# Gated linear attention in an already tuned two-layer trunk: value products of 512 columns, attention products set among the projections, two levels with fewer key columns

## The chip, the cores and the metric

The kernel runs on one core of a Trainium2 chip. The metric is the device time of one execution in microseconds (us), as the median of several runs; the profile is one further execution, recorded by the hardware profiler.

## The reference

A trunk of two layers works on 512 tokens of width 1024, all in float32. Each layer has a token mixer and a gated convolutional feed-forward network (FFN, inner width 2816); around every sublayer stand an RMS norm of the input with a shift and scale (adaLN) and an RMS norm of the output with a gate. Layer 0 mixes tokens with an RG-LRU recurrence, layer 1 with gated linear attention (GLA), which is what the change touches:

```python
proj = h @ w_in
q, k, v, r, z = jnp.split(proj, [GLA_QK, 2 * GLA_QK, 2 * GLA_QK + D_MODEL, 2 * GLA_QK + 2 * D_MODEL], axis=-1)
log_alpha = jax.nn.log_sigmoid((z @ w_alpha + b_alpha)) / GLA_TAU
...
o_inter = jnp.einsum('bhcd,bhde->bhce', qc * jnp.exp(big_g), state)
attn = jnp.einsum('bhid,bhjd,bhijd->bhij', qc, kc, decay)   # decay = exp(G_i - G_j), causal
o_intra = jnp.einsum('bhij,bhje->bhie', attn, vc)
state = jnp.exp(g_last)[..., None] * state + jnp.einsum('bhjd,bhje->bhde', kc * jnp.exp(g_last - big_g), vc)
...
o = rmsnorm(o, norm_g)
return (o * jax.nn.silu(r)) @ w_out
```

There are four heads, with keys of 128 and values of 256.

## The kernel before, in words

Activations lie with channels on the 128 partitions and the 512 tokens along the free axis; `h` is eight tiles of 128 by 512. For accuracy every large product is done three times in the type float32r: the weight and the activation are each split into a high and a low part, and hi·hi, hi·lo and lo·hi are summed in PSUM (`mm3`, `mms`). Weights come from memory in units of 512 KB (`unit`, `load_upto`): a DMA of the SP queue into one of 3 raw slots, a cast on ScalarE (`acopy`, L416), a subtraction on VectorE (`tt`, L364), and the two parts lie in one of 8 slots of the pool `w`. Most other tiles come from a pool `g` of 43 slots; products go to 7 PSUM banks, `mm`.

Before it emits anything the program records all its operations and orders them with a list schedule in Python (`Sched.order`). TensorE takes the lowest recorded operation whose inputs are ready by the schedule's own reckoning, so it goes in recorded order except where something isn't ready; the other engines go by the longest path to the end. How long an operation takes in this reckoning is written in `Emit`: for products in `mms`. At run time each engine executes its list strictly in order and waits on semaphores. So a number in `mms` can move instructions in the whole program, not only in GLA.

In GLA, the projections of z, q and k come first. Then for each head in turn: a product for the diagonal of the 128 by 128 attention blocks (`diag_start`); the value projection (`vproj`), which holds 128 tokens of `h` stationary and moves 256 weight columns, 96 products; two blocks of the output gate `r` (`rproj`), which hold the weights and move 512 tokens, 48 products; seven levels of the decayed attention (`level_x` prepares on VectorE and ScalarE, `level_mm` multiplies four token blocks, in plain float32, and `masked` copies the result under a mask); the products between blocks (`inter_mm`); and `attend`, which multiplies attention and values and norms the result. A plain float32 product stands in the order once and in the profile twice, since the chip runs it in two passes.

Each output projection (`out_proj`) runs the two token halves one after the other and norms each: `rstd_bcast` sums squares over partitions with a product of one column per 128 tokens ("the sum", tile `nr`), computes the power on POOL, puts it on a diagonal on VectorE and broadcasts it by one more product (also `nr`, "the broadcast"). This happens for y and, with the next sublayer's input in view, for h: four norms per `out_proj`, whose two products each stand somewhere among the products of the other half. `h_tile` then makes the next input, and the next sublayer's first products need it (`proj_halves`).

Of the kernel before, what the change touches and what calls it, by code (L numbers as in the profile page):

```python
# [12 lines left out]
ALU = mybir.AluOpType  # L13
# [16 lines left out]

def unit_list():
    """Weight units in the order of their use: (key, array name, [(k, m), ...])."""
# [42 lines left out]
# column-parameter layout  # L75
# [10 lines left out]
class Buf:  # L86
    """A tile whose place on the chip is taken when its first instruction is emitted."""
# [10 lines left out]
class View:  # L98
# [41 lines left out]
class Sched:  # L140
    """Records the kernel's instructions with their operands, orders them by a list schedule
    (deadlines from the longest path to the end, the tensor engine in program order), and
    emits them to Tile in that order."""
# [34 lines left out]
    def order(self):  # L178
# [23 lines left out]
        # allocation order per class  # L202
# [29 lines left out]
        cand = {e: [] for e in ENGS}     # (prio, idx) ready or soon ready  # L232
        wait = {e: [] for e in ENGS}     # (ready, idx)
# [11 lines left out]
        while done < n:  # L245
# [8 lines left out]
            for e in ENGS:  # L254
# [7 lines left out]
                if e == "act" and cand[e]:  # L262
                    # a change of the function table costs time: prefer the present one
# [80 lines left out]
class Emit:  # L344
    """Instruction wrappers: costs and operands for the schedule, closures for the emission."""
# [118 lines left out]
def trunk(ctx, tc, xT, wall, adaT, par_d, c_d, walpha_d, ident_d, masks_d, outT):  # L464
# [57 lines left out]
    def load_upto(i):  # L522
        while nxt[0] <= min(i, len(UNITS) - 1):
# [9 lines left out]
            if UNITS[j][0] in ingen:  # L533
                # in general tiles, which are plenty at the start of a sublayer
# [8 lines left out]
            if UNITS[j][0][0] == "gz":  # L543
                # 16 columns of either part side by side: one product serves both
# [44 lines left out]
    def rstd_from(nr, nt, dim, act=False):  # L589
        """nr[:, :nt]: sums per token tile -> rstd broadcast to all partitions (PSUM)."""  # L590
# [38 lines left out]
    def mod_cols(layer, part, k0=0, k1=KD):  # L629
        """Finish a part: 0/3 shift, 1/4 (1+scale)*norm_g, 2/5 gate*norm_g."""  # L630
# [32 lines left out]
    def h_tile(h, k, sl, rb, n, layer, part_sh):  # L663
        """h = (x * s2) * rstd + shift, in two parts."""
# [7 lines left out]
    def out_proj(src, wkey, klist, gate, nexth, yacc=None):  # L672
        """Last product of a sublayer, y = src @ W (+ yacc); x += gate * rmsnorm(y) * g; then the
        next sublayer's h, or the output. The token halves follow each other, so that the norms
        of one run beside the products of the other."""
# [4 lines left out]
        for sl in HALVES:  # L680
            acc = s.buf("gh", F32, 256)
            ys = []
            for m in range(KD):
# [28 lines left out]
            if nexth is None and sl is HALVES[1]:  # L712
                # the tensor engine, idle by now, takes part of the sums
# [35 lines left out]
    def proj_halves(keys, h_):  # L749
        """First products of a sublayer, by token halves and input tiles as these become ready."""  # L750
# [79 lines left out]
    def ada_col(part, k):  # L830
        """One column of the first norm's shift or scale."""
# [419 lines left out]
```

## Time and profile before

| | |
|---|---|
| median of 3 runs | 1185.19 us (1184.75 to 1185.59) |
| span of the profiled execution, first to last instruction | 1182.5 us |
| TensorE busy | 1158.9 us, 98% of the span |
| VectorE, ScalarE busy | 867.3 us (73%), 553.6 us (47%) |
| granted TensorE clock, mean | 0.999 |
| GLA's value, gate and attention products | 608 to 756 us of the span |

The profiled execution's own time is not listed apart from its span; the median lies 2.7 us above the span. A row of the timeline reads: start, length, engine, line, operation, tiles written and read, the stationary block (rows*columns), the moving one, and how many follow each other; a matmul's end is modelled, so the distance of two starts says more than a length.

### The profile page before, as it was taken

The numbers are of one execution on the slowest core, as the hardware profiler recorded it, in microseconds if no ns is written. First come the engines' busy times: TensorE is split into PE (matmuls) and PEld (weight loads), VectorE is DVE, ScalarE is ACT, GpSimd is POOL, SyncE is SP. The second block draws the span as 40 slices with busy tenths as digits, with TensorE's granted clock in tenths as the row PEclk, the third lists the DMA queues.
The fourth block names the chain that finished last, engine by engine and source line by source line (L and its number), as shares of the span: only waits on it lengthen the run. The fifth ranks groups of instructions, "written<-read, shape, count | busy, mean of one in ns | idle before, by whom it ended". The sixth has DMA issues, their size and how long they took to land.

```text
span 1182.5 us, 16970 instructions
## 1 busy us (share of the span) xinstructions
PE 1158.9 (98%) x6664; PEld 1017.0 (86%) x6664; DVE 867.3 (73%) x1470; ACT 553.6 (47%) x874; POOL 24.4 (2%) x37
## 2 busy tenths in 40 slices
PE   4999999999999999999999999999999999999998
PEld 3878899988888888899999899999988888888897
DVE  7999999988988956558779767458845556645635
ACT  5688864743333324434478344254643333424421
POOL 1000001000000000000000000000000000000000
PEclk9999999999999999999999999999999999999999
DMA  8956562477787843232412211203243333332202
GB/s 338 312 170 202 200 214 73 160 249 252 249 260 223 261 126 93 88 90 59 144 55 90 72 54 55 72 27 118 72 125 97 100 91 105 90 107 90 72 1 72
DMA packets 45857, 157.44 MB, mean 133 GB/s; under 512 B 4977, under 2 KB 7281, under 8 KB 45778
## 3 DMA queue, kind: packets, MB, share of 16 engines
q1 hardware_dynamic: 45778, 156.36, 41.6%
q8 instruction: 52, 0.85, 0.3%
q14 instruction: 27, 0.22, 0.1%
HBM read 154.25 MB, written 2.10 MB: 132 GB/s over the span
## 4 chain that ended last, share of the span: by engine, by line
PE 90%; DVE 5%; ACT 3%; issue 1%; DMA 1%; SPq 0%; POOL 0%; DVEq 0%; POOLq 0%
PE mm L435 88%; ACT g L411 2%; PE nr L435 1%; DVE g L377 1%; DVE w L364 1%; ACT L411 1%; DVE g L364 1%; ACT w L416 1%; DVE gh L377 1%; DVE g L393 1%; DVE w L377 1%; DMA const<-in_xT_dram 0%; DMA raw<-in_wall_dram 0%; DVE araw L377 0%; SPq L441 0%
## 5 line engine op out<-in xcount | busy, mean ns | idle before, releaser
L435 PE MATMUL mm<-g,w 128*128 128x512 f32 (+1 forms) x5114 | 957.5, 348 | 5.6 <-ACT g L416 2.5
L435 PEld LDWEIGHTS mm<-g,w 128*128 128x128 f32 x5114 | 826.2, 189 | 130.4 <-ACT g L416 4.1
L364 DVE TENSOR_TENSOR w<-raw,w 128x1024 fp32r<-128x1024 f32 (+1 forms) x181 | 217.8, 1205 | 152.4 <-ACT w L416 152.0
L416 ACT CAST w<-raw 128x1024 fp32r<-128x1024 f32 (+1 forms) x181 | 187.2, 1036 | 206.3 <-PE mm L435 202.3
L377 DVE SCALAR_TENSOR_TENSOR g<-mm,const,g 128x511 f32<-128x511 f32 (+3 forms) x208 | 153.3, 745 | 11.2 <-ACT g L411 5.3
L364 DVE TENSOR_TENSOR g<-g,g 128x512 f32<-128x512 f32 (+4 forms) x213 | 126.2, 614 | 37.7 <-ACT g L411 19.4
L411 ACT ACTIVATE g<-mm,const 128x512 f32<-128x512 f32 (+1 forms) x148 | 102.2, 698 | 20.6 <-PE mm L435 20.5
L411 ACT ACTIVATE g<-g 128x512 f32<-128x512 f32 (+1 forms) x132 | 66.7, 540 | 96.2 <-DVE g L377 77.4
L435 PE MATMUL mm<-g,g 128*128 128x256 f32 (+4 forms) x748 | 102.1, 293 | 0.0
L435 PEld LDWEIGHTS mm<-g,g 128*128 128x128 f32 (+1 forms) x748 | 94.8, 191 | 3.8
L416 ACT CAST g<-g 128x512 fp32r<-128x512 f32 (+1 forms) x74 | 45.4, 614 | 107.7 <-DVE g L364 105.0
L377 DVE SCALAR_TENSOR_TENSOR araw<-araw,const 128x1024 f32<-128x1024 f32 x72 | 87.1, 1220 | 9.2 <-DMA araw<-in_adaT_dram 9.0
L364 DVE TENSOR_TENSOR g<-g,mm 128x512 f32<-128x512 f32 (+1 forms) x80 | 44.9, 577 | 44.5 <-PE mm L435 44.2
L364 DVE TENSOR_TENSOR gh<-gh,gh 128x256 f32<-128x256 f32 x97 | 40.4, 420 | 22.2 <-ACT gh L411 20.6
L435 PE MATMUL mm<-w,g 128*128 128x256 f32 x384 | 49.6, 288 | 0.0
L435 PEld LDWEIGHTS mm<-w,g 128*128 128x128 f32 x384 | 46.9, 192 | 1.4 <-issue 1.4
L368 POOL TENSOR_TENSOR sm<-sm,const 128x2 f32<-128x2 f32 (+1 forms) x19 | 19.4, 1022 | 1025.7 <-DVE sm L388 1018.5
L411 ACT ACTIVATE gh<-g 128x256 f32<-128x256 f32 x32 | 13.1, 416 | 51.3 <-DVE g L364 51.3
L411 ACT ACTIVATE g<-gh,const 128x256 fp32r<-128x256 f32 x48 | 21.9, 503 | 26.4 <-DVE gh L377 26.2
L411 ACT ACT_TABLE_LOAD x24 | 30.8, 1283 | 1.1 <-PEq L1242 0.7
L377 DVE SCALAR_TENSOR_TENSOR w<-w,const 128x1024 f32<-128x1024 f32 x24 | 28.8, 1217 | 0.0
L411 ACT ACTIVATE gh<-const 128x256 f32<-128x256 f32 x48 | 18.9, 414 | 20.1 <-DVE const L364 20.0
(66 smaller groups left out, 465.6 us busy)
## 6 DMA issues: line engine op xcount, KB each, us to landing
raw<-in_wall_dram SPq DMA_DIRECT2D x186, 512.0 KB, 3.7
araw<-in_adaT_dram SPq DMA_DIRECT2D x72, 512.0 KB, 4.5
w<-in_adaT_dram SPq DMA_DIRECT2D x24, 512.0 KB, 5.8
raw<-in_wall_dram SPq DMA_DIRECT2D x8, 384.0 KB, 6.7
const<-in_xT_dram SPq DMA_DIRECT2D x8, 256.0 KB, 4.1
out_dram<-const SPq DMA_DIRECT2D x8, 256.0 KB, 2.1
araw<-in_masks_dram SPq DMA_DIRECT2D x1, 512.0 KB, 5.2
const<-in_par_dram SPq DMA_DIRECT2D x1, 291.0 KB, 3.6
```

The source lines that it names most:

```text
L364: self.s.add(eng, dur, lambda: e.tensor_tensor(out.ap(), a.ap(), b.ap(), op=op), [a, b], [out])
L368: lambda: self.nc.gpsimd.tensor_tensor(out.ap(), a.ap(), b.ap(), op=ALU.pow), [a, b], [out])
L377: return self.nc.vector.scalar_tensor_tensor(out.ap(), a.ap(), f(sc), b.ap(), op0=op0, op1=op1, **kw)
L393: lambda: self.nc.vector.tensor_tensor_scan(out.ap(), a.ap(), b.ap(), 0.0, op0=ALU.mult, op1=ALU.add),
L411: return self.nc.scalar.activation(out.ap(), a.ap(), func, **kw)
L416: self.s.add("act", (0.095 if self._sb(a) else 0.052) + out.n * 0.8325e-3, lambda: self.nc.scalar.copy(out.ap(), a.ap()), [a], [out])
L435: r.append(self.nc.tensor.matmul(g[0].ap(), g[1].ap(), g[2].ap(), start=g[3], stop=g[4], **kw))
```

## The change

The value weights of two heads are laid side by side: a `gv` unit holds two input tiles by four column tiles, four units serve a pair of heads, and `vproj` makes one token block of 128 for both heads with products that move 512 columns. It holds the same `h` blocks stationary. A list, `GLA_CHUNKS`, fixes the order of 16 projections of 24 products each (8 of values, 8 of the gate); each head takes the next 6, 3, 5 and 2 of them, and its nine small steps (diagonal, seven levels, the products between blocks) are recorded evenly behind these. `level_mm` and `masked` leave out key columns that the mask clears anyway where that leaves 96 or fewer: 96 of 128 at level 32, 64 of 128 at level 64. `mms` charges other times: 11 ns more for each float32r product, and for plain float32 a time that depends on the columns moved and held. Comments are dropped, and lines are shifted by 6.

```diff
+GLA_CHUNKS = ([("v", t) for t in range(4)] + [("r", 0), ("r", 1), ("r", 2), ("r", 3), ("v", 4), ("v", 5),
+              ("v", 6), ("v", 7), ("r", 4), ("r", 5), ("r", 6), ("r", 7)])
+GLA_ENDS = (6, 9, 14, 16)
...
-    for h in range(NH):
-        for half in range(2):
-            u.append((("gv", h, half), "gla_w_in",
-                      [(4 * half + k, 8 + 2 * h + c) for k in range(4) for c in range(2)]))
-        for j in range(2):
-            u.append((("gr", 2 * h + j), "gla_w_in", [(k, 16 + 2 * h + j) for k in range(KD)]))
+    for what, i in GLA_CHUNKS:
+        if what == "r":
+            u.append((("gr", i), "gla_w_in", [(k, 16 + i) for k in range(KD)]))
+        elif i % NT == 0:
+            for quarter in range(4):
+                u.append((("gv", i // NT, quarter), "gla_w_in",
+                          [(2 * quarter + k, 8 + 4 * (i // NT) + c) for k in range(2) for c in range(4)]))
...
             if g[1].buf.dt == FR:
-                dur += max(n, 256) * 0.4167e-3 + 0.0025
+                dur += max(n, 256) * 0.4167e-3 + 0.0135
             else:
-                dur += max(n, 118 if n > 1 else 100) * 1.667e-3 + 0.005
+                dur += 2 * max(n * 0.8333e-3 + 0.002, 0.112 if g[1].n > 64 else 0.062)
...
+    def vproj(pair, t):
+        w = [unit("gv", pair, i) for i in range(4)]
+        ps = mmtile()
+        for k in range(KD):
+            ww, c = w[k // 2], (k % 2) * S
+            hh, hl = h[k]
+            whi, wlo = ww[c:c + S], ww[D + c:D + c + S]
+            tok = tsl(t)
+            e.mms([(ps[:], hh[tok], whi, k == 0, False), (ps[:], hl[tok], whi, False, False),
+                   (ps[:], hh[tok], wlo, False, k == KD - 1)])
+        vt[pair, t] = gt()
+        e.acopy(vt[pair, t][:], ps[:])
...
-        e.mms([(ps[t * n:(t + 1) * n], xt[tsl(t)], part3(xt[tsl(t)], 2 * hb, hb, 2 * hb), True, True)
-               for t in range(NT)])
-        masked(atd, lv, ps, 2 * hb, hb)
+        rows = P - hb
+        rows = rows if rows <= 96 else P
+        e.mms([(ps[t * n:(t + 1) * n].rows(rows), xt[t * P:t * P + rows], part3(xt[tsl(t)], 2 * hb, hb, 2 * hb),
+                True, True) for t in range(NT)])
+        masked(atd, lv, ps, 2 * hb, hb, rows)
...
     for hd in range(NH):
-        atd = diag_start(hd)
-        vproj(hd)
-        sr = rproj(hd)
-        for lv, hb in enumerate(LEVELS):
-            level_mm(atd, lv, level_x(hd, hb))
-        ax = inter_mm(inter_x(hd))
-        attend(hd, atd, ax, sr)
+        ats, axs = {}, {}
...
+        small = [start] + [lambda lv=lv: level(lv) for lv in range(len(LEVELS))] + [inter]
+        chunks = GLA_CHUNKS[done:GLA_ENDS[hd]]
+        done = GLA_ENDS[hd]
+        given = 0
+        for n, (what, i) in enumerate(chunks):
+            vproj(i // NT, i % NT) if what == "v" else rproj(i)
+            upto = len(small) * (n + 1) // len(chunks)
+            for f in small[given:upto]:
+                f()
+            given = upto
+        attend(hd, ats[0], axs[0])
```

The first place is TensorE in GLA's first head. Before, the seven levels follow each other behind the second gate projection (the row of 128x512); the row's last figures are the output block.

```order
L435 MATMUL mm_5923<-g_5152,w_5478 128x512
L435 MATMUL mm_5973<-g_5717 128x64 x4
L435 MATMUL mm_5980<-g_5725 128x64 x4
L435 MATMUL mm_5988<-g_5734 128x64 x4
L435 MATMUL mm_5995<-g_5759 128x64 x4
L435 MATMUL mm_6005<-g_5781 128x64 x4
L435 MATMUL mm_6013<-g_5795 128x64 x4
L435 MATMUL mm_6021<-g_5819 128x64 x4
L435 MATMUL mm_6033<-g_5761,g_5832 128x128
```

Now level 32 stands alone between two gate projections:

```order
L441 MATMUL mm_5977<-g_5172,w_5587 128x512
L441 MATMUL mm_5977<-g_5132,w_5587 128x512
L441 MATMUL mm_6016<-g_5764 96x64 x4
L441 MATMUL mm_6025<-g_5005,w_5615 128x512
L441 MATMUL mm_6025<-g_5022,w_5615 128x512
```

What moved: the levels stand in 14 groups behind a longer product in the four heads together, where they stood in 4; three of the groups are level 64 or begin with it, two begin with level 32.

The second place is TensorE where the first FFN ends and GLA's first products begin (rows of 32x256 are the product with the weights of z, the first that needs GLA's `h`; the `nr` row is the last norm's broadcast). Before, six products stand between the two:

```order
L435 MATMUL nr_5342<-gh_5367,const_82 128x256
L435 MATMUL mm_5138<-g_5142,w_4890 128x256
L435 MATMUL mm_5138<-g_5171,w_4890 128x256
L435 MATMUL mm_5138<-g_5142,w_4890 128x256
L435 MATMUL mm_5138<-g_5152,w_4890 128x256
L435 MATMUL mm_5138<-g_5181,w_4890 128x256
L435 MATMUL mm_5138<-g_5152,w_4890 128x256
L435 MATMUL mm_5098<-g_5028,w_4801 32x256
```

Now there are 24; the broadcast is followed by

```order
L441 MATMUL nr_5335<-gh_5360,const_82 128x256
L441 MATMUL mm_5149<-g_5126,w_4853 128x256
L441 MATMUL mm_5149<-g_5167,w_4853 128x256
L441 MATMUL mm_5149<-g_5126,w_4853 128x256
L441 MATMUL mm_5149<-g_5132,w_4853 128x256
L441 MATMUL mm_5149<-g_5172,w_4853 128x256
L441 MATMUL mm_5149<-g_5132,w_4853 128x256
L441 MATMUL mm_5155<-g_5077,w_4896 128x256
```

What moved: the norm's two products came forward past other work. The same holds before the first FFN: between the last broadcast of a half and the first product that needs `h`, 6 products became 36 in the first half and 12 became 30 in the second. Between the sum and the broadcast of the eight norms of the first two output projections stood 27, 24, 21, 24, 18, 18, 25 and 21 products; now 21, 18, 21, 18, 15, 18, 20 and 18.

The third place is VectorE in head 0, where the second pair's value weights are split (rows with `raw`; `COPY_PREDICATED` is a level's masked copy):

```order
L370 TENSOR_TENSOR w_5945<-raw_5637,w_5945 128x1024
L370 TENSOR_TENSOR w_5955<-raw_5689,w_5955 128x1024
L1078 COPY_PREDICATED g_5778<-const_5654,mm_5958 128x32x8
L1078 COPY_PREDICATED g_5778<-const_5654,mm_5968 128x16x16
L370 TENSOR_TENSOR w_5963<-raw_5853,w_5963 128x1024
L370 TENSOR_TENSOR w_6004<-raw_5966,w_6004 128x1024
L1078 COPY_PREDICATED g_5778<-const_5654,mm_6016 96x8x32
```

What moved: the four units of a pair are split together; these four stand among the copies of head 0, and the product that first reads one of them stands behind the attention of head 0 and two more gate projections. Before, two units of the next head stood about there.

More of the change, by code (lines that the diff above doesn't have):

```diff
@@ L1066, in bcol, with masked @@
         return v.map(lambda a: a.rearrange("p (n c) -> p n c", c=c)[:, :, j:j + 1].to_broadcast([P, v.n // c, c]))
-    def masked(atd, lv, ps, c, lo):
+    def masked(atd, lv, ps, c, lo, rows=P):
         def cut(v, t):
-            return v.ap().rearrange("p (t n c) -> p t n c", t=t, c=c)[:, :, :, lo:c]
+            return v.ap()[0:rows].rearrange("p (t n c) -> p t n c", t=t, c=c)[:, :, :, lo:c]
         n, k = P // c, c - lo
@@ L1075, in masked @@
         e.dve(0.07 + src.n * 1.042e-3, lambda: nc.vector.copy_predicated(
-            cut(atd[:], NT), cut(masks[lv * P:(lv + 1) * P], 1).to_broadcast([P, NT, n, k]),
-            src.ap().rearrange("p (t n c) -> p t n c", t=NT, c=k)),
+            cut(atd[:], NT), cut(masks[lv * P:(lv + 1) * P], 1).to_broadcast([rows, NT, n, k]),
+            src.ap()[0:rows].rearrange("p (t n c) -> p t n c", t=NT, c=k)),
             [atd[:], masks[lv * P:(lv + 1) * P], src], [atd[:]])
@@ L1133, in inter_mm, with rproj, attend @@
         return axa, axb
-    def rproj(hd):
-        sr = []
-        for j in range(2):
-            ps = mmtile()
-            proj(ps, unit("gr", 2 * hd + j), h)
-            t = gt()
-            e.act(t[:], ps[:], AF.Tanh, scale=0.5, table="exp")
-            e.stt(t[:], t[:], 1.0, ps[:], ALU.add, ALU.mult)
-            sr.append(t)
-        return sr
-    def attend(hd, atd, ax, sr):
+    sr = {}
+    def rproj(j):
+        ps = mmtile()
+        proj(ps, unit("gr", j), h)
+        t = gt()
+        e.act(t[:], ps[:], AF.Tanh, scale=0.5, table="exp")
+        e.stt(t[:], t[:], 1.0, ps[:], ALU.add, ALU.mult)
+        sr[j] = t
+    def attend(hd, atd, ax):
         axa, axb = ax
@@ L1170, in attend, with level, start, inter @@
             e.stt(t[:], pos[d2][:], hng[d2:d2 + 1], rs[:], ALU.mult, ALU.mult)
-            e.tt(t[:], t[:], sr[d2][:], ALU.mult)
+            e.tt(t[:], t[:], sr[2 * hd + d2][:], ALU.mult)
             osp[2 * hd + d2] = split(t)
+    done = 0
     for hd in range(NH):
-        atd = diag_start(hd)
-        vproj(hd)
-        sr = rproj(hd)
-        for lv, hb in enumerate(LEVELS):
-            level_mm(atd, lv, level_x(hd, hb))
-        ax = inter_mm(inter_x(hd))
-        attend(hd, atd, ax, sr)
+        ats, axs = {}, {}
+        def level(lv, hd=hd, ats=ats):
+            level_mm(ats[0], lv, level_x(hd, LEVELS[lv]))
+        def start(hd=hd, ats=ats):
+            ats[0] = diag_start(hd)
+        def inter(hd=hd, axs=axs):
+            axs[0] = inter_mm(inter_x(hd))
+        small = [start] + [lambda lv=lv: level(lv) for lv in range(len(LEVELS))] + [inter]
[9 more added lines that the diff above has]
+        attend(hd, ats[0], axs[0])
     h = new_h()
```

20 lines of the change are left out of this document (2 added, 18 removed).

## The prediction

> **What bounds the kernel now.** I read the page first, then a table of GLA's four heads, then TensorE's timeline there and at the norms.
>
> ```profile
> span 1182.5 us, 16970 instructions
> ...
> PE 1158.9 (98%) x6664; PEld 1017.0 (86%) x6664; DVE 867.3 (73%) x1470; ACT 553.6 (47%) x874; POOL 24.4 (2%) x37
> ...
> PE 90%; DVE 5%; ACT 3%; issue 1%; DMA 1%; SPq 0%; POOL 0%; DVEq 0%; POOLq 0%
> ```
>
> TensorE (PE) is busy for 98% and holds 90% of the chain of waits. The stretches of the four heads, 37 us each:
>
> ```profile
> 608.00:645.00 37.00, 37.00 (x264) 34.43 (x263) 35.88 (x66) 33.94 (x63) 0.53 (x1) 1.00 0.23 71
> 645.00:682.00 37.00, 37.00 (x257) 33.72 (x256) 26.60 (x52) 14.41 (x28) 2.58 (x2) 1.00 0.18 59
> 682.00:719.00 37.00, 37.00 (x260) 34.00 (x259) 26.21 (x52) 15.07 (x31) 1.64 (x2) 1.00 0.21 58
> 719.00:756.00 37.00, 37.00 (x260) 33.99 (x259) 23.02 (x44) 15.19 (x28) 1.12 (x1) 1.00 0.30 86
> ```
>
> The columns are the length, then PE, PEld, DVE, ACT and POOL busy, then the granted clock. PE never rests, at the full clock of 1.00: what PE's products save here, the kernel saves, and small steps set between projections fill no hole, because there is none. VectorE (DVE) has 10 us to spare per head, but only 1.1 in the first.
>
> **The products, from starts.** Head 0 and two plain rows:
>
> ```profile
> 608.96 11.76 PE L435 MATMUL mm<-w,g 128*128 128x256 f32 x96
> 620.55 11.07 PE L435 MATMUL mm<-g,w 128*128 128x512 f32 x48
> 631.46 6.36 PE L435 MATMUL mm<-g 128*128 128x64 f32 x56
> 637.66 2.45 PE L435 MATMUL mm<-g,g 128*128 128x128 f32 x20
> ...
> 197.23 6.64 PE L435 MATMUL mm<-g,g 128*128 128x256 f32 x54
> 203.71 0.50 PE L435 MATMUL nr<-const,gh 128*128 128x1 f32 x4
> ```
>
> 256 columns: (203.71 - 197.23)/54 = 0.120 us. 512 columns: (631.46 - 620.55)/48 = 0.227 us. Doubling the columns costs 0.107; 0.013 per product is fixed. The 384 value products become 192: 384 x 0.120 - 192 x 0.227 = 46.1 - 43.6 = **2.5 us** less. The weights' 8 units, their splits and the evacuated columns are as many as before, beside PE.
>
> The Trainium skill ("TensorE: Matmul & The Clock Gate", section "Wait — 56ns, not 53.3ns?") gives warm products N/2.4 ns plus about 2.5: 109.2 and 215.8 ns, by which widening would save 0.5 us and the whole sum come to 4.3. The rows above show 120 and 227 and disagree; the measurement decides.
>
> The levels: 56 passes take 637.66 - 631.46 = 6.20 us, 0.111 each, for 64 moving columns. What spaces them is the load of the stationary block, and a load with fewer columns is shorter:
>
> ```profile
> L435 PEld LDWEIGHTS mm<-g,w 128*128 128x128 f32 x437 | 69.1, 190 | 9.6 <-issue 0.5
> ...
> L435 PEld LDWEIGHTS mm<-g 128*128 128x128 f32 x224 | 25.6, 192 | 0.3
> ...
> L435 PEld LDWEIGHTS mm<-g,w 128*32 128x32 f32 x27 | 2.9, 108 | 1.7 <-ACT g L411 0.9 <-DVE g L377 0.5
> ```
>
> (192 - 108)/96 columns = 0.875 ns per column: 56 ns less at 64, 28 less at 96. A pass can't go below its streaming, which the first pass behind a long product shows, its load being done:
>
> ```profile
> 631.46 0.22 PE L435 MATMUL mm<-g 128*128 128x64 f32 x1
> ...
> 631.52 0.38 PE L435 MATMUL mm<-g 128*128 128x64 f32 x2
> ```
>
> That is 0.058. So level 64: 4 heads x 8 passes x (0.111 - 0.058) = **1.7 us**; level 32: 32 x 0.028 = **0.9 us**, bounded below by 0 if only halves of the block count. I take the slope, which both its ends measure. VectorE's masked copies keep their columns, so nothing changes there.
>
> Spreading: each group behind a longer product has one pass at 0.058 in place of 0.111. The 14 such groups were 4; three begin with level 64 (already 0.058, gain 0), two with level 32 (0.025 each), so 5 more at 0.053 and 2 at 0.025: **0.3 us**, from 0 up.
>
> **What the moved steps need.** I cost the move at nothing else, so its cover has to be named. In head 0 the first levels now come behind the diagonal and two value projections, at about 608.2 + 0.9 + 2 x 5.45 = 620, eleven us earlier than 631.46. Their inputs are made on VectorE in this stretch (a subtraction of 512 columns for each level and one more for the products between blocks; the pieces of 256 between them are the decayed queries and keys):
>
> ```profile
> 609.65 1.89 DVE L364 TENSOR_TENSOR g<-g 128x512 f32<-128x512 f32 x3
> 611.46 1.09 DVE L364 TENSOR_TENSOR g<-g,g 128x256 f32<-128x256 f32 x3
> ...
> 617.22 0.68 DVE L364 TENSOR_TENSOR g<-g 128x512 f32<-128x512 f32 x1
> ```
>
> The eighth and last subtraction starts at 617.22, before PE would ask for the first level; the later levels are asked for one or two at a time, 5.45 us apart. The two heads that have the fewest projections are the second (3) and the fourth (2). For the fourth, PE has 2 x 5.45 for the gates, 0.9 for the diagonal, 5.5 for the levels and 1.4 between blocks, 18.7 us, and VectorE needs the 23.0 of its row above. What covers the difference is that VectorE works ahead: the first head's attention now stands behind four value and two gate projections, 32.7 us of them where 22.5 stood (11.6 + 10.9 in the rows above), so VectorE, with the same work, has ten us more until then, and keeps a part of that lead. If the lead were gone, because the pool `g` of 43 tiles holds four value tiles per pair of heads where two per head were held, the fourth head would wait 23.0 - 18.7 = 4.3 us; the sum would still be a gain. The writes to PSUM are no new limit: a value projection fills one bank and ScalarE empties it in one copy, as two halves of a bank were filled and emptied before. POOL and SP do the same operations as before, and the SP queue loads the same 512 KB units, in the order in which the planner wants them.
>
> **The new order outside GLA.** The new durations in the planner bring the norms' products forward. That can win where PE waits for the next sublayer's `h`:
>
> ```profile
> 184.92 1.06 PE L435 MATMUL mm<-g,w 128*128 128x256 f32 x6
> 186.39 0.38 PE L435 MATMUL mm<-g,w 128*128 128x256 f32 x1 [0.40 <-ACT g L411]
> 187.03 0.86 PE L435 MATMUL mm<-g,w 128*128 128x256 f32 x5 [0.26 <-DVE g L377]
> ...
> 207.27 1.78 PE L435 MATMUL mm<-g,g 128*128 128x256 f32 x12
> 208.89 0.28 PE L435 MATMUL mm<-g,w 128*128 128x256 f32 x1
> 209.38 0.86 PE L435 MATMUL mm<-g,w 128*128 128x256 f32 x5 [0.22 <-DVE g L377]
> ...
> 574.58 0.70 PE L435 MATMUL nr<-gh,const 128*128 128x256 f32 x2
> 574.93 1.06 PE L435 MATMUL mm<-g,w 128*128 128x256 f32 x6
> 576.64 0.30 PE L435 MATMUL mm<-g,w 128*32 128x256 f32 x1 [0.65 <-ACT g L411]
> 577.28 0.30 PE L435 MATMUL mm<-g,w 128*32 128x256 f32 x1 [0.34 <-DVE g L377]
> ```
>
> Beyond 0.120 per product the starts are late by 0.75 and 0.52, by 0.18 and 0.37, by 0.99 and 0.52: 3.3 us. From the broadcast to the first `h` product passed 2.06 us (574.58 to 576.64); 24 products behind the broadcast now last 2.88, and 30 and 36 do at the other places. These waits should go: 3.3 us.
>
> It can lose at the norms themselves, whose products may now come before their input:
>
> ```profile
> 207.03 0.59 PE L435 MATMUL nr<-gh,const 128*128 128x256 f32 x2
> ...
> 206.13 0.48 DVE L388 TENSOR_SCALAR gh<-const,sm 128x128 f32<-128x128 f32 x2 [0.59 <-POOL sm L368]
> ...
> 573.94 0.59 DVE L388 TENSOR_SCALAR gh<-const,sm 128x128 f32<-128x128 f32 x2 [0.59 <-POOL sm L368]
> ```
>
> At 207.03 the diagonal was done at 206.61, 0.42 to spare; six products fewer are 0.72, so 0.30 late. At 574.58 it was done at 574.53, 0.05 to spare; three fewer are 0.36, so 0.31 late. By the same count some eight norm products go beyond their spare, by about 0.3 each: 2.4 us, an estimate from these two. I take 3.3 - 2.4 = **0.9 us** gained, between 3.3 gained and 2.4 lost.
>
> **The sum**: 2.5 + 1.7 + 0.9 + 0.3 + 0.9 = 6.3 us. The span of 1182.5 becomes 1176.2; the median stands 2.7 above the span, so 1185.2 - 6.3 = **1178.9 us**. With all bounds at their best (8.7) 1176.5, at their worst (2.5 + 1.7 - 2.4 = 1.8) 1183.4.
>
> **The rivals.**
>
> *The norms come too early.* Nothing is won at `h` because the whole chain (sum, POOL, VectorE, broadcast) only waits elsewhere: 5.4 - 2.4 = 3.0, 1182.2 us. For it: the two spares above are smaller than the shift. Against: many products still stand between, and where PE waits at a norm, `h` still comes earlier.
>
> *The trimmed blocks save nothing*, if the spacing of float32 passes is something else than the load: 6.3 - 2.6 = 3.7, 1181.5 us. For it: the short loads in the trace belong to float32r products of 256 columns, which hide any load. Against: the load's own length, 108 and 192.
>
> *Slower: the value weights come late.* A pair's first projection, 24 x 0.227 = 5.45 us, now needs four units within it, the fourth after 4.1 us. The splits:
>
> ```profile
> L364 DVE TENSOR_TENSOR w<-raw,w 128x1024 fp32r<-128x1024 f32 (+1 forms) x181 | 217.8, 1205 | 152.4 <-ACT w L416 152.0
> L416 ACT CAST w<-raw 128x1024 fp32r<-128x1024 f32 (+1 forms) x181 | 187.2, 1036 | 206.3 <-PE mm L435 202.3
> ```
>
> If four splits only began with that projection, they would take 1.04 + 4 x 1.21 = 5.9 us alone and 11.8 where VectorE gives them half its time, as in the crowded first head: a wait of 7.7, net 1.4 slower, 1186.6 us. It decides from 6.3 us of wait on. Against: the second pair's splits stand among the copies of head 0, far ahead of their use.
>
> **How the numbers follow.** Forecast 0.65, norms too early 0.18, no gain from trimming 0.12, late weights 0.05. A measurement of this kernel can tell about 0.2%, 2.4 us: faster means under 1182.8. The forecast is faster almost surely (0.64), the second case two times in three (0.12), the third nearly always (0.10), the last never: faster 0.86, same 0.11, slower 0.03. The range runs from the best bound to just above the second case: 1176.6 to 1182.8.
>
> **What would show it.** 6472 PE products, the value ones x24 of 128x512 with starts 0.227 apart; passes of level 64 0.058 apart and of level 32 0.083; loads of 136 and 164 ns for 64 and 96 columns; no idle time marked at GLA's first `h` product; waits of about 0.3 at some `nr` products. I am wrong if PE waits inside GLA between projections and levels, if the trimmed passes stay at 0.111, or if a wait of over 1 us appears at any norm.

## The result: 17.6 us slower, and where the profile shows it

The changed kernel takes 1202.57 us (median of 4, 1200.91 to 1203.23) against 1184.97 for the kernel before on the same chip: a ratio of 1.0145, 95% interval 1.0131 to 1.0160. The forecast was 1178.9. The profiled execution spans 1200.5 us against 1182.5. The page of the changed kernel, its first lines and the chain of waits:

```profile
span 1200.5 us, 16581 instructions
...
PE 1162.0 (97%) x6472; PEld 1008.5 (84%) x6472; DVE 870.8 (73%) x1470; ACT 551.7 (46%) x873; POOL 26.5 (2%) x37
...
PE 61%; DVE 22%; DMA 9%; issue 4%; ACT 2%; POOL 1%; SPq 0%; DVEq 0%; POOLq 0%; ACTq 0%
```

TensorE has its 6472 products, 192 fewer than before, but is busy for 3 us more and holds 61% of the chain instead of 90%; VectorE and DMA hold 31% where they held 6%. GLA's four heads, now 18 us later (length, PE, PEld, DVE, ACT, POOL busy, granted clock):

```profile
626.00:663.00 37.00, 37.00 (x194) 31.56 (x193) 34.11 (x61) 32.97 (x58) 0.00 (x0) 1.00 0.18 59
663.00:700.00 37.00, 37.00 (x221) 31.35 (x220) 24.38 (x46) 12.52 (x23) 1.64 (x2) 1.00 0.22 71
700.00:737.00 37.00, 37.00 (x209) 31.57 (x208) 27.28 (x55) 16.65 (x33) 1.64 (x2) 1.00 0.19 57
737.00:774.00 37.00, 36.02 (x241) 31.34 (x239) 28.10 (x56) 16.92 (x34) 1.64 (x2) 1.00 0.17 58
```

Here PE rests for 1 us, in the fourth head. The loss is elsewhere. The start of the same-numbered PE product in both traces gives how late the changed kernel is (behind GLA's heads the number is less by the 192 products that it does not have):

| up to (us in the trace before) | late by | added in this part |
|---|---|---|
| 32, first norm | 2.7 | 2.7 |
| 142, end of the RG-LRU's projections | 2.7 | 0 |
| 158, begin of its output projection | 11.8 | 9.1 |
| 210, that output projection | 13.7 | 1.9 |
| 370, first part of the first FFN | 17.3 | 3.6 |
| 595, end of that FFN, GLA's first projections | 18.2 | 0.9 |
| 769, GLA's heads | 16.2 | -2.0 |
| 828, GLA's output projection | 18.0 | 1.8 |

PE's timeline of the changed kernel shows the waits that make these steps (in brackets the idle time before and what ended it):

```profile
20.54 2.04 PE L441 MATMUL nr<-g,const 128*128 128x512 f32 x2 [5.06 <-DVE g L394]
...
160.05 2.29 PE L441 MATMUL mm<-g,w 128*128 128x256 f32 x9 [8.12 <-DVE w L370]
...
191.00 0.58 PE L441 MATMUL nr<-const,gh 128*128 128x1 f32 x4 [0.56 <-DVE gh L370]
194.43 0.70 PE L441 MATMUL nr<-gh,const 128*128 128x256 f32 x2 [0.60 <-DVE gh L394]
...
379.99 10.24 PE L441 MATMUL mm<-g,w 128*128 128x512 f32 x44 [2.19 <-DVE g L383]
```

The first of these waits was 3.16 before and the second 0.8; the others were not there. Of the 2.7 us of the first step, 1.4 stand by the start of the products at 25.24 (23.81 before). The other 1.3 come from products of 256 columns that start 0.213 us apart instead of 0.120: up to 31 us there are 25 of them, before only 11, and between 11 and 26 in the traces of all kernels here, so these 1.3 need not be the order's. The second, 8.12 us, ends when VectorE has split the first weight unit of the RG-LRU's output projection. Within it the clock is halved, as a table of stretches of the changed kernel shows (granted clock third from the end):

```profile
152.00:160.00 8.00, 0.00 (x0) 0.00 (x0) 8.00 (x12) 3.35 (x5) 0.00 (x0) 0.62 0.20 68
160.00:162.00 2.00, 1.95 (x9) 1.95 (x10) 2.00 (x3) 0.00 (x0) 0.00 (x0) 0.50 0.46 104
162.00:164.00 2.00, 2.00 (x11) 2.00 (x11) 1.47 (x2) 0.88 (x3) 0.00 (x0) 0.50 0.79 211
164.00:166.00 2.00, 2.00 (x18) 2.00 (x17) 1.71 (x4) 1.85 (x6) 0.00 (x0) 0.97 0.80 303
```

The step of 9.1 us is 7.3 of more waiting and the rest, 1.8, of half clock behind the wait, up to about 164.

**Why the split came late.** VectorE starts the fourth of the recurrence's eight scans at nearly the same time in both traces, and the last two 8.9 us later after the change. Before:

```profile
108.03 1.22 DVE L393 TENSOR_TENSOR_SCAN g<-g,g 128x512 f32<-128x512 f32 x1
...
146.42 2.33 DVE L393 TENSOR_TENSOR_SCAN g<-g,g 128x512 f32<-128x512 f32 x2
```

After:

```profile
108.12 1.22 DVE L399 TENSOR_TENSOR_SCAN g<-g,g 128x512 f32<-128x512 f32 x1
...
155.34 2.34 DVE L399 TENSOR_TENSOR_SCAN g<-g,g 128x512 f32<-128x512 f32 x2
```

Between them the groups of instructions agree, except for the adaLN multiplications (one row of a modulation matrix times the conditioning vector; each has a 512 KB load into one of two `araw` slots or a `w` slot). Groups of the kernel before, 109.2 to 146.4 us (count, busy, mean ns, idle time before):

```profile
L377 DVE SCALAR_TENSOR_TENSOR araw<-araw,const 128x1024 f32<-128x1024 f32 x7 | 8.3, 1219 | 0.0
L377 DVE SCALAR_TENSOR_TENSOR w<-w,const 128x1024 f32<-128x1024 f32 x5 | 5.9, 1219 | 0.0
```

The changed kernel, 109.3 to 155.3 us:

```profile
L383 DVE SCALAR_TENSOR_TENSOR araw<-araw,const 128x1024 f32<-128x1024 f32 x9 | 10.9, 1224 | 4.0 <-DMA araw<-in_adaT_dram 4.0
L383 DVE SCALAR_TENSOR_TENSOR w<-w,const 128x1024 f32<-128x1024 f32 x7 | 8.4, 1222 | 0.2 <-DMA w<-in_adaT_dram 0.2
```

Sixteen instead of twelve: four times 1.15 (from start to start) is 4.6 us, and VectorE waits 4.2 us for their data; together the 8.8. The stretches are 37.2 and 46.0 us. The chain of waits has the two late loads (start, time from issue to landing):

```profile
139.18 4.38 DMA araw<-in_adaT_dram
...
144.92 5.63 DMA araw<-in_adaT_dram
```

The planner reckons 2.0 - 0.75 + 1.46 (512 KB) + 0.9 = 3.6 us for such a load, and 0.45 for its issue. On the chip VectorE stood in its list behind data that was still under way, with the scans and the weight split behind it.

**The same ahead of 380.** In the first FFN, from 358 to 377 us, VectorE waits three times for adaLN loads (1.02, 0.67 and 0.94 us; in the same part of the trace before once, 0.91). Weight splits stand behind them, and the operations on line 383 that read products (`g<-mm`), one of which ends TensorE's wait of 2.19 us at 380. The last of the three:

```profile
376.03 1.23 DVE L383 SCALAR_TENSOR_TENSOR araw<-araw,const 128x1024 f32<-128x1024 f32 x1 [0.94 <-DMA araw<-in_adaT_dram]
```

### The profile page after: what moved, and what is told of

It is laid out like the page before. It is cut to its first block, busy times and chain, and to the rows that moved or that the text cites. A ratio compares the mean times of both kernels' runs of the same rounds, so it can differ in the third digit from the quotient of the medians.

```text
span 1200.5 us, 16581 instructions
## 1 busy us (share of the span) xinstructions
PE 1162.0 (97%) x6472; PEld 1008.5 (84%) x6472; DVE 870.8 (73%) x1470; ACT 551.7 (46%) x873; POOL 26.5 (2%) x37
## 4 chain that ended last, share of the span: by engine, by line
PE 61%; DVE 22%; DMA 9%; issue 4%; ACT 2%; POOL 1%; SPq 0%; DVEq 0%; POOLq 0%; ACTq 0%
PE mm L441 60%; DMA araw<-in_adaT_dram 7%; DVE g L383 4%; DVE g L370 4%; DVE w L370 3%; DVE gh L370 3%; DVE araw L383 3%; DMA raw<-in_wall_dram 2%; DVE w L383 1%; DVE gh L383 1%; DVE const L370 1%; PE nr L441 1%; ACT g L417 1%; POOL sm L374 1%; DVE g L399 1%
## 5 line engine op out<-in xcount | busy, mean ns | idle before, releaser
L383 DVE SCALAR_TENSOR_TENSOR g<-mm,const,g 128x511 f32<-128x511 f32 (+2 forms) x208 | 153.6, 746 | 15.5 <-ACT g L417 7.7
L417 ACT ACTIVATE g<-mm,const 128x512 f32<-128x512 f32 (+1 forms) x148 | 101.8, 696 | 16.2 <-PE mm L441 16.1
L441 PE MATMUL mm<-w,g 128*128 128x512 f32 x192 | 46.8, 397 | 0.0
L441 PEld LDWEIGHTS mm<-w,g 128*128 128x128 f32 x192 | 35.4, 188 | 7.5 <-issue 0.5
L422 ACT COPY g<-mm 128x512 f32<-128x512 f32 (+1 forms) x36 | 19.7, 559 | 24.4 <-PE mm L441 24.4
L417 ACT ACTIVATE gh<-const 128x256 f32<-128x256 f32 x48 | 19.2, 415 | 21.8 <-DVE const L370 21.6
```

Of the source, the lines that this page charges most:

```text
L383: return self.nc.vector.scalar_tensor_tensor(out.ap(), a.ap(), f(sc), b.ap(), op0=op0, op1=op1, **kw)
L417: return self.nc.scalar.activation(out.ap(), a.ap(), func, **kw)
L422: self.s.add("act", (0.095 if self._sb(a) else 0.052) + out.n * 0.8325e-3, lambda: self.nc.scalar.copy(out.ap(), a.ap()), [a], [out])
L441: r.append(self.nc.tensor.matmul(g[0].ap(), g[1].ap(), g[2].ap(), start=g[3], stop=g[4], **kw))
```

## The experiments

The difference to 1185.0 us (the kernel before, in each set of runs between 1184.97 and 1185.26) is what counts. All kernels compute the whole reference except the one that says otherwise.

### The planner's durations against the change of GLA

Four kernels exchange the two figures in `mms`: the changed kernel with both old ones, the kernel before with both new ones, and the changed kernel with one new figure each. The first:

```
-                dur += max(n, 256) * 0.4167e-3 + 0.0135
+                dur += max(n, 256) * 0.4167e-3 + 0.0025
-                dur += 2 * max(n * 0.8333e-3 + 0.002, 0.112 if g[1].n > 64 else 0.062)
+                dur += max(n, 118 if n > 1 else 100) * 1.667e-3 + 0.005
```

> The whole change, but the planner keeps the old durations of products (float32r 0.0025, plain float32 as before), so that the order ahead of GLA is the order before. Theory 1 (the loss comes from the order that the new durations make, ahead of GLA): the 18.2 us that the changed kernel has lost by its first value product are not lost, and what it wins in GLA's products (about 3 us by the two traces) stays: 1181 to 1183 us. Rival (the loss comes from the GLA parts themselves, which use memory and buffers otherwise): the time stays near 1202. Third (half and half): 1190 to 1195.

> The kernel before with nothing changed but the two durations in the planner; every instruction is one of the kernel before. Theory 1: slower by the 18 us that were lost ahead of GLA, 1200 to 1206 us, with the wait of about 8 us near 155 us of the span. Rival: 1185.

> The whole change with the new duration for plain float32 products and the old one for float32r. If the float32r figure (11 ns more on nearly 5900 products) is what tilts the order: near e1, 1181 to 1186 us. If any change of a duration reshuffles the order by chance: anything between 1180 and 1205, with losses at other places than in the changed kernel.

> The whole change with the new duration for float32r products and the old one for plain float32. If the float32r figure tilts the order: near the changed kernel, 1195 to 1204 us, with the long wait near 155 us. If by chance: anything between 1180 and 1205.

| | float32r figure | float32 figure | us | ratio to before (95%) |
|---|---|---|---|---|
| change, old durations | 0.0025 | old | 1181.73 | 0.9973 (0.9963 to 0.9984) |
| change, float32 new | 0.0025 | new | 1186.70 | 1.0015 (1.0006 to 1.0024) |
| change, float32r new | 0.0135 | old | 1200.95 | 1.0136 (1.0121 to 1.0151) |
| the change | 0.0135 | new | 1202.57 | 1.0145 (1.0131 to 1.0160) |
| before, new durations | 0.0135 | new | 1212.94 | 1.0235 (1.0218 to 1.0252) |

With the old durations the order ahead of GLA is that of before, and the change of GLA gains 3.3 us. The same figures put into the kernel before, GLA untouched, cost 28 us: 9.28 us of wait at 160.60, and 2.29 at 658.25 among the grouped levels. That is more than the 18 us expected there. So the loss is the planner's, and most of it comes from 11 ns more per float32r product: that figure alone costs 19.2 us against the run with both old ones. The float32 figure costs 5.0 alone, just past its expected range, and 1.6 on top of the other. The long wait at the first norm belongs to the float32 figure: 5.06 us in the three kernels of the table that have it new, 3.17 in the other two. Where it is long, VectorE has five more small operations and a weight split of 0.96 us ahead of the norm's diagonal.

### What the parts of GLA's change are worth

In the changed kernel with the old durations, once the trimming is taken out (`rows = P`), once the spreading:

```
-            upto = len(small) * (n + 1) // len(chunks)
+            upto = 1 if n + 1 < len(chunks) else len(small)
```

> The change with the planner's old durations and without the trimming: levels 32 and 64 hold and copy all 128 keys again (mms order differs in no place but the tile names). Against 1181.7 for the change with the old durations. Prediction's terms (level 64: 1.7 us, level 32: 0.9 us): 1184.3. Rival from the trace after, where a pass of level 64 is 0.053 us shorter but the way out of such a group into a product of 512 columns is some 0.06 longer and the way in 0.09 longer: level 64 gains about 0.8 and level 32 about 0.8, so 1183.3. If the trimming saves nothing at all: 1181.7.

> The change with the planner's old durations, trimmed, values in products of 512, but in each head only the diagonal stands behind the first projection and all levels behind the last one, as before the change. Against 1181.7. The prediction gave spreading 0.3 us: 1182.0. Rival: every separate group costs 0.06 us on the way out and up to 0.09 on the way in, which the shorter first pass does not repay; ten groups fewer then save about 1 us: 1180.8. If VectorE needs the projections to prepare the levels, PE waits at the levels of the heads with few projections: later than 1183, with idle time before the 64 column products.

Without trimming 1182.78 us: it saves 1.05, between nothing and the rival's 1.6. The heads of GLA, by starts, gain 3.5 us with it and 2.3 without. Without spreading 1187.68: 5.95 more, the third case of the expectation. PE's timeline in the fourth head without spreading:

```profile
743.61 1.08 PE L441 MATMUL mm<-g 128*128 128x64 f32 x8 [1.41 <-DVE g L1078]
745.20 6.00 PE L441 MATMUL mm<-g 128*128 128x64 f32 x32 [0.52 <-DVE g L394]
751.13 2.93 PE L441 MATMUL mm<-g,g 128*128 128x128 f32 x12
753.72 2.08 PE L441 MATMUL mm<-g,w 128*128 128x256 f32 x9
755.63 4.55 PE L441 MATMUL mm<-g,g 128*128 128x384 f32 x28
```

The same groups with spreading and the old durations:

```profile
742.96 3.18 PE L441 MATMUL mm<-g 128*128 128x64 f32 x32
746.07 1.60 PE L441 MATMUL mm<-g,g 128*128 128x128 f32 x12
747.43 1.31 PE L441 MATMUL mm<-g,w 128*128 128x256 f32 x9
748.58 4.55 PE L441 MATMUL mm<-g,g 128*128 128x384 f32 x28
```

Two waits of 1.93 us together, and behind them 32 passes in 5.93 instead of 3.11, 12 products in 2.59 instead of 1.36, 9 in 1.91 instead of 1.15: 4.8 us more, at half clock. With the waits that is 6.7 of the 7.1 us by which the spans differ (1186.5 and 1179.4). In this order of projections spreading is cover for VectorE, a need which the prediction had named and had costed at nothing.

### Where the new durations hurt

The first run has the new durations for products recorded from GLA on and the old ones ahead of it. The second is the whole change with all loads landing 1.5 us later in the plan; its diff:

```
-                    o.end = dma_free + 0.9
+                    o.end = dma_free + 2.4
```

> The whole change, but the planner's new durations are used only for products recorded from GLA on; ahead of it the old ones stand. The order ahead of GLA's own products is that of the run with the old durations. Theory (the loss lies in the order that the new durations make ahead of GLA): 1181 to 1183, all of the 18 to 21 us of difference to the changed kernel gone. Rival (the new durations cost wherever they are used, since the waits in GLA at 763 and 773 us come from them too): 1184 to 1187.

> The changed kernel with all its new durations, but the planner lets every load land 1.5 us later (2.4 us behind the transfer in place of 0.9), since the adaLN loads that VectorE waits for took 4.4 and 5.6 us where the planner reckons 3.6. Theory (the right durations of the products are harmless; the harm is that VectorE's list sets adaLN multiplications ahead of their data and of the weight split): the 8.1 us wait at 160 us falls below 3 us and the time to 1190 or less. Rival (the old order was the result of a search with the old figures, and any other order is some 10 to 20 us worse): 1195 to 1205, with waits at other places.

In GLA only: 1185.01. Of the 18 to 21 us all but 3.3 are gone, but more is left than the theory allowed; it is the rival's range. By starts 1.5 us of the heads' gain are lost, with waits of 0.63 and 0.36 in the fourth head, and 2.7 in GLA's output projection, where the waits are at the norms, as the prediction's rival "The norms come too early" had it. Two of its four:

```profile
805.95 0.58 PE L443 MATMUL nr<-const,gh 128*128 128x1 f32 x4 [0.49 <-DVE gh L371]
...
810.07 0.70 PE L443 MATMUL nr<-gh,const 128*128 128x256 f32 x2 [0.56 <-DVE gh L395]
```

With later landings: 1189.66, the wait at 152 is 2.26 us instead of 8.12. All new durations are in it, and 12.9 of the 17.6 us are back. The rival (any other order is 10 to 20 us worse) falls: this order is another one, 4.6 us worse than the kernel before.

The next two lengthen the norm's power on POOL by 0.9 us in the plan, once with each of these: in GLA alone on top of the first, everywhere on top of the second, whose diff is

```
-        self.s.add("pool", 0.3 + 0.165 * out.n,
+        self.s.add("pool", 1.2 + 0.165 * out.n,
```

> As the run with the new durations in GLA only (1185.0), and in GLA the planner takes the norm's power on POOL 0.9 us longer: from the start of that power to the diagonal on VectorE passed 1.58 us at 807.95 to 809.53 there, where the planner reckons 0.69 for two columns. Theory (with shorter products the plan covered too short a chain of the norm by too many products; with right products the chain's own figure must be right too): the waits at the norms between 790 and 820 us (1.6 us in the four) go, time 1183.4 or less, and 1181.7 as with the old durations if the wait at 745 goes as well. Rival (the waits have another cause, VectorE's splits ahead of the norm's small operations in its list): no change, 1184.5 to 1186.

> The changed kernel with all new durations, landings 1.5 us later and every norm's power 0.9 us longer in the planner. Theory: the norms' waits of the run with later landings alone (0.48, 0.67, 0.24, 0.55, 0.20, 0.45, 0.31, 0.33, 0.22: 3.4 us) go, from 1189.7 to 1186.3, and to 1184 if the half clock that follows the wait at 152 goes too. If the waits at the norms come from VectorE's order: 1189 to 1191.

Both expectations missed: 1188.85 and 1202.50. The waits at GLA's norms did become smaller (1.6 to 0.9 us), but the longer figure moved VectorE's other work: in the first a wait of 1.99 us came at 672.57 for a masked copy, with some 6 us of half clock behind it; in the second the first norm waits 6.2 us instead of 5.0 and the split at 156 3.8 instead of 2.3, both followed by more. A truer figure for one operation was no better here.

### VectorE's stretch ahead of the output projection, taken apart

The changed kernel in its own order, 16 adaLN products cut to 64 of 1024 columns (left incomplete):

```
+        if 21 < nada[0] <= 37:
+            s.add("dve", 0.07 + D * 1.042e-3, lambda: nc.vector.scalar_tensor_tensor(
+                raw[0:64].ap(), raw[0:64].ap(), 1.0, cact[0:64].ap(), op0=ALU.mult, op1=ALU.mult,
+                accum_out=acc.ap()), [raw, cact[:]], [raw, acc])
...
```

> The changed kernel in its own order, but 16 adaLN products of VectorE (the 22nd to the 37th, those between the second and the fourth pair of the recurrence) multiply 64 of their 1024 columns, so their result is left incomplete; their loads are whole. It takes 16 x 1.07 = 17 us of VectorE's time out of the stretch. Theory A (VectorE's time decides: four more such products between the third-last and the last scans than before, 4.6 us): the wait at 160 us goes from 8.1 to under 1, time 1191 or less. Theory B (the landings decide: each load waits for one of two slots and takes 4.4 to 5.6 us, so a series of such products can't go faster than one in 2.5 us): VectorE only waits longer for the loads, and the wait on PE stays above 4 us, time 1196 or more.

1199.04 us, the wait 3.15 us instead of 8.12, so neither theory alone: 5 us of the wait go with VectorE's time, and the other 3 stay although about 15 us of work (15 products at 1.0) were taken out ahead of the split, since VectorE then waits for the loads (2.3 and 0.6 us) and for ScalarE (1.1, 1.1 and 0.9). The time shows 3.5 of these 5 us; a wait of 1.00 us at a norm of GLA's output projection is new.

And the whole change with only the adaLN loads later in the plan, by 2.5 us:

```
...
-        e.load(raw, adaT[layer, jt], P * D * 4)
+        e.load(raw, adaT[layer, jt], P * D * 4, late=2.5)
```

> The changed kernel with all its new durations, but the planner lets the adaLN loads alone land 2.5 us later. TensorE's list differs from the change's in 31 of 6037 rows; between the second and the fourth pair of scans VectorE's holds 13 adaLN products instead of 16. Theory (these products, set ahead of their data and of the weight split, cause the wait at 160 us): wait there 3 us or less instead of 8.1, time 1192 to 1195.5, the other waits of the change as they are (start 2, norms, 380). Rival (VectorE is bound there whatever it does first): wait above 6 us, 1199 or more.

1193.53 us, inside the range of the theory:

```profile
154.63 5.61 PE L441 MATMUL mm<-g,w 128*128 128x256 f32 x30 [2.84 <-DVE w L370]
```

TensorE's list is nearly that of the change, and 9.0 of the 17.6 us are gone with the place of these multiplications in VectorE's list. By starts the step at the split falls from 9.1 to 3.8 us, and that between 210 and 370 from 3.6 to nothing: the wait of 2.19 us at 380 is gone too, so it had the same cause. In the execution that was profiled, at 1196.23, a wait of 1.74 us came at a norm of GLA's output projection, with half clock behind it; the other three took 1193.1 to 1193.8.

### The loss against the figure

The changed kernel, float32 duration old, with other fixed parts for a float32r product; the last has the adaLN loads 2.5 us later as well:

```
-                dur += max(n, 256) * 0.4167e-3 + 0.0135
+                dur += max(n, 256) * 0.4167e-3 + 0.006
```

> The change with the old duration for plain float32 and 0.006 us for the fixed part of a float32r product, between the old 0.0025 (1181.7) and the new 0.0135 (1200.95). If the loss grows with the figure: about 1187.8 (0.0035 of 0.011 of 19.2 us). If any other order than that of the old figures is hurt alike (a search found that one): 1190 to 1200. If it takes a threshold (VectorE's order between the last pairs of scans holds 14 adaLN products here, 12 with the old figures, 16 with the new): no wait above 1 us at 150 to 160 and 1182 to 1185.

> As the run with 0.006, with 0.004 us for the fixed part of a float32r product. If the loss grows with the figure: 1181.7 to 1182. If the orders scatter: anything from 1180 to 1190, with a wait of some 2 us near 152 as at 0.006, since VectorE's list holds 14 adaLN products between those scans as there.

> As the run with 0.006, with 0.009. VectorE's list between the last pairs of scans holds 14 adaLN products as at 0.006; the norms come earlier than there. If the loss grows evenly from 0.006 (1182.0) to 0.0135 (1201.0): 1189.6. If the large part of it is the 16 adaLN products: 1184 to 1187, with waits of 0.2 to 0.6 us at the norms and no wait above 3 us at 150 to 160.

> As the run with 0.006 (1182.0: no wait for h at 186, 209 and 577, 0.3 us of waits at norms, but 2.8 us at 153 and half the clock behind it), and the adaLN loads alone land 2.5 us later in the plan; TensorE's list differs in 23 rows. Theory: the wait at 153 falls to 1 us or less and the half clock goes: 1182.0 - 1.8 - 1.7 = 1178.5, which is the forecast of the change with its gain outside GLA. Rival: the wait stays or goes to another place, 1181 to 1184.

| figure | adaLN products between the fourth and the last two scans | wait for the split at 150 to 158 | other waits over 0.1 us between 160 and 600 | us |
|---|---|---|---|---|
| 0.0025 | 12 | 0.72 | at `h`: 0.41, 0.26, 0.22, 0.65, 0.33 | 1181.73 |
| 0.004 | 14 | 1.33 | at `h`: 1.23, 0.50, 0.31 | 1182.37 |
| 0.006 | 14 | 2.82 | at norms: 0.11, 0.20 | 1182.04 |
| 0.009 | 14 | 3.91 | at norms: 0.34, 0.19, 0.12 | 1186.70 |
| 0.0135 | 15 | 7.94 | nine at norms, 0.15 to 0.67; three at 367 to 378, together 3.3 | 1200.95 |

The wait for the split grows with the figure all along. The waits at `h` go, as predicted, and then norms take their place. By the medians, what is won up to 0.006 pays for the split. In the profile at 0.006 it does not: the split's step costs 3.9 us, the parts behind it win 1.7, and that execution took 1183.92, where the seven lie between 1180.33 and 1183.92. At 0.009 the split's step costs 4.6 and the parts behind still win 1.0; at 0.0135 both lose. Neither expectation on waits held: at 0.006 the time of the third case came with a wait of 2.82 us, at 0.009 the lower time with one of 3.91. The row at 0.006:

```profile
153.33 6.91 PE L441 MATMUL mm<-g,w 128*128 128x256 f32 x40 [2.82 <-DVE w L370]
```

With the adaLN loads later in the plan this wait does fall to 0.78 us, but by 142 us the products start 3.0 us later than at 0.006, 1.1 of it in products 0.213 us apart at the start, and the waits for `h` are back (0.46, 0.80, 0.67 and 0.26): 1185.46, slower than even the rival's 1184. No version here has both ends. The change with the old durations, 1181.73, and the one with 0.006, 1182.04 (ratio 0.9972, 0.9961 to 0.9983), are 0.3% faster than the kernel before.

## Why the prediction was wrong

**The step that failed** is "The new order outside GLA", + 0.9 us between 3.3 gained and 2.4 lost; the stages outside GLA's heads cost 20 us by starts, 18.2 ahead of them and 1.8 behind. The prediction had quoted that the planner's numbers can move instructions in the whole program, and then priced two kinds of places on PE: the norms and the waits for `h`. It did not follow VectorE's list in the RG-LRU stage, where VectorE, not PE, sets when the first output product can start, and where four more multiplications with late loads now stand ahead of the weight split: 9.1 us there, and 3.6 where the same happens in the first FFN. The list of "What would show it" named a wait over 1 us at a norm; the 8.1 us came at a weight split.

**Waits for `h`**: mechanism right, size smaller. At 0.006, where all five go, the parts around them win 0.3 and 1.4 us by starts (from 4.77 late to 4.47, and from 4.45 to 3.09), 1.7 of the 3.3, less 0.3 of waits at norms that came with it.

**Norms too early**: right in kind, and not a rival but a part of what came. Five waits of 0.23 to 0.60 us stand in the first output projection, three of 0.21 to 0.58 in the second, where about eight of 0.3 were estimated.

**Value products, 2.5 us**: right. The timeline of the changed kernel's first head:

```profile
626.35 5.60 PE L441 MATMUL mm<-w,g 128*128 128x512 f32 x24
631.79 1.05 PE L441 MATMUL mm<-g,g 128*128 128x128 f32 x8
...
639.84 5.73 PE L441 MATMUL mm<-w,g 128*128 128x512 f32 x24
645.41 1.00 PE L441 MATMUL mm<-g 128*128 128x64 f32 x8
646.22 5.70 PE L441 MATMUL mm<-w,g 128*128 128x512 f32 x24
...
659.00 0.81 PE L441 MATMUL mm<-g 128*96 128x64 f32 x8
659.62 5.73 PE L441 MATMUL mm<-g,w 128*128 128x512 f32 x24
665.28 0.68 PE L441 MATMUL mm<-g 128*64 128x64 f32 x8
665.89 1.60 PE L441 MATMUL mm<-g,g 128*128 128x128 f32 x12
```

24 products take 631.79 - 626.35 = 5.44 us, 0.227 each. With the old durations the heads gain 3.5 us by starts, and less the trimming's 1.05 that leaves 2.5 for values and spreading together.

**Trimming, 2.6 us**: 1.05 measured. The loads do have the predicted length (groups of PEld, mean ns):

```profile
L441 PEld LDWEIGHTS mm<-g 128*96 128x96 f32 x32 | 3.2, 165 | 0.9 <-PE mm L441 0.7
L441 PEld LDWEIGHTS mm<-g 128*64 128x64 f32 x32 | 2.2, 137 | 1.1 <-issue 1.1
```

The passes too are spaced as predicted, 0.085 and 0.058 us. Level 32 takes 0.62 us from its first pass to the next product, a full level 0.81: 0.19 for 8 passes, where 0.22 was predicted. Level 64 takes 0.61: 0.20 where 0.42 was predicted, and the 24 products ahead of it take 5.66 us instead of 5.57 ahead of a full level. The step at fault is "8 passes x (0.111 - 0.058)": it counted all eight steps of a group as equal. In a full level the first step is 0.055 already, and the one out into the next product 0.084; at level 64 these two are 0.106 and 0.153, in all four heads.

**Spreading, 0.3 us**: wrong in kind. The shorter first passes are paid back (24 products between two levels take 5.57 instead of 5.44), and the spreading's worth is in the waits that it avoids, 5.95 us in the experiment.

**Value weights late** did not come: no PE wait for a value weight is in the trace. What stays open is by which step of its reckoning the planner moves the adaLN multiplications when the figures change, and why the norms of the output projections wait as much as they do with each figure; for these only the waits were read, no cause was tested.

## What to carry to other kernels

Where a planner orders in-order engines, changing a duration is a change of the whole program: compare the order of every engine, above all in the stage where another engine than the fast one sets the pace, and price what now stands ahead of the instruction that releases the next stage. A truer figure for one engine can be worse while the figures beside it (here the landing of loads) stay wrong: with later landings in the plan 9.0 and 12.9 of the 17.6 us came back. That the old errors had offset each other is a reading of this, not shown. Change the work and the planner's figures in separate steps, and measure each.

## What the runs showed of the hardware that was not expected

Of 19 waits of TensorE of 1.0 to 2.8 us in these traces, behind the first 30 us, 12 were followed by a stretch at half clock and 7 were not. Three stretches (granted clock third from the end): the float32 figure alone new, where a wait of 2.20 us ended at 152.30;

```profile
152.30:154.00 1.70, 1.70 (x13) 1.70 (x14) 1.70 (x3) 0.00 (x0) 0.00 (x0) 0.94 0.45 55
154.00:156.00 2.00, 2.00 (x12) 2.00 (x11) 2.00 (x3) 1.39 (x4) 0.00 (x0) 0.50 0.68 244
```

later landings, where one of 2.26 us ended at 152.47;

```profile
152.40:156.00 3.60, 3.53 (x29) 3.54 (x30) 3.60 (x6) 1.67 (x6) 0.00 (x0) 1.00 0.52 155
```

and the kernel without spreading, after 1.41 and 0.52 us, among passes of 64 columns.

```profile
745.20:754.00 8.80, 8.80 (x45) 8.56 (x46) 7.20 (x15) 1.20 (x2) 0.00 (x0) 0.50 0.01 2
```

So waits of 2 us can cost 2 us or 7. By the granted clock such a stretch lasted 3.4 us among products of 256 and 512 columns, and 6.8 (three times) or 10.2 us (once) among the levels; in some of them it began before the wait was over. The Trainium skill ("TensorE: Matmul & The Clock Gate", section "Part 1: The HAM clock gate (the "warmup" mystery)") has the clock halved after at least one idle window of about 3.4 us, with windows that run free of the kernel. The lengths agree, one, two or three times 3.4 us. The idle time does not: the shorter waits show that less than a window of it is enough here, and in the wait of 8.12 us, which began at 151.94, the granted clock was 1.00 up to 153.80 and 0.50 from 154.00. That the windows run free may be why of two waits of 2.2 us only one was followed by half clock, which no run here tests.
